# Newton steps of the FFN norms on VectorE, and pools that wait per tile, in a two-layer MLA/NSA decoder trunk

## The chip, the cores and the metric

The kernel runs on one core of a Trainium2 chip. A core has five engines that each work through a queue of their own in order: TensorE (PE, matmuls into PSUM banks), VectorE (DVE), ScalarE (ACT), GpSimd (POOL) and SyncE (SP, which here issues transfers). The metric is the device time of one execution in microseconds (us); the median of the runs before is 1926.41 us.

## The reference

The reference is a decoder trunk of depth 2 on one sequence of 512 tokens and 1024 channels, in float32. Each layer is

```
h = h + 0.5 * swiglu(rmsnorm(h, g_a), w_gate, w_up, w_down)
h = h + mixer(rmsnorm(h, g_m))
h = h + 0.5 * swiglu(rmsnorm(h, g_b), w_gate, w_up, w_down)
```

with `swiglu(x) = (silu(x @ w_gate) * (x @ w_up)) @ w_down` (2816 hidden channels) and `rmsnorm(x, g) = x * rsqrt(mean(x * x) + 1e-6) * g`. The mixer of layer 0 is multi-head latent attention (MLA, 16 heads), that of layer 1 native sparse attention (NSA: compressed, selected and sliding-window branches with gates and a relative bias). A last rmsnorm follows.

## The kernel before, in words

The hidden state lies in SBUF with channels on the partitions, as eight chunks `h` of 128 x 512. Six stages follow each other: FFN, MLA, FFN, FFN, NSA, FFN. Every float32 matmul is made of three matmuls on a high and a low part of each operand (L162 to L164, L364 to L366, L352 to L354 by stage). So every weight slab is loaded by SP into a buffer `wr` or `ru`, copied to a high part `w` by ACT (L143, L170) and its low part is made by DVE as the difference (L145, L171), or by POOL in the attention loops (L149). The slabs `w` have two buffers.

An FFN stage (`ffn`) computes the first three blocks of 128 hidden channels plainly (`plain`, two slabs each, gate into `pg` and up into `pu`), and the other 19 blocks by a scheme with seven products on combined operands (`combine` makes the combined inputs `four` from `h` with the operations L232, L236 to L238 and L171; `wsums` makes the sums of weights). The down projection runs in units of three blocks whose weights are `wd` (L407, L170, L171); the last four blocks are the tail, after which each chunk's square sum is added (L250 on ACT, L254 on POOL) and its input to the next stage is split (L173, L174).

The channel norm is not applied to the input of the matmuls; its factor per token, `row`, multiplies their results. It is made so: `norm_col` (L278) sums the squares over the partitions by four small matmuls into `pc`; `rsqrt` makes an estimate by three DVE steps (L259 to L261) and refines it by three Newton rounds on a tile of 128 x 4; `norm_bcast` (L290) spreads the result over all partitions by eight small PE instructions into `pb`; ACT copies `pb` to `row` (L450 in the FFN), and the gates `tg` are multiplied with it (L377). In the FFN `pb` stands in PE's order behind the second plain block. The Newton rounds of `rsqrt` have two forms:

```
for _ in range(3):
    if pool:
        nc.gpsimd.tensor_tensor(t, y, y, op=ALU.mult)                                # L264
        nc.gpsimd.tensor_tensor(t, t, v, op=ALU.mult)                                # L265
        nc.gpsimd.tensor_scalar(t, t, -0.5, 1.5, op0=ALU.mult, op1=ALU.add)          # L266
        nc.gpsimd.tensor_tensor(y, y, t, op=ALU.mult)                                # L267
        continue
    nc.vector.scalar_tensor_tensor(t, y, -0.5, v, op0=ALU.mult, op1=ALU.mult)        # L269
    nc.vector.tensor_tensor(t, t, y, op=ALU.mult)                                    # L270
    nc.vector.scalar_tensor_tensor(y, t, 1.5, y, op0=ALU.add, op1=ALU.mult)          # L271
```

The first FFN gets its square sums from token rows that ACT squares (L422), the others from `norm_col`. The norms of MLA and NSA call `rsqrt` without `pool`.

Tiles come from pools. Pools that live throughout hold `h`, the inputs (`x`, `four`), the weight slabs and small things; each stage opens pools of its own and releases them at its end: `act` and `ft` in an FFN, `mla` and `mlat` in MLA, `nsa`, `nsaq`, `cmp` (compression of keys and values, released inside the stage) and then `nsat` in NSA. Pools of a later stage lie on the bytes of earlier ones. `cmp` holds the bias table `btab` and its source `tb`, the positions `pos` (copied to `xc`, L950), the compression weights `w1` and `w2` (L962, L974), the hidden values and `vc`, which POOL copies into `vcm` (L1012). `nsat` holds `npth` and `nptl`, `th` (bias rows `cb`, L1031, and `th`, L1081, loaded from the table in DRAM), `e` (scores plus bias, L1038, transposed by PE into `ptc`, L1043), `p` and the outputs. The compressed scores `sc` are made at L1035 and L1036.

The program is recorded in the order of the Python code; the compiler then orders each engine's queue from a model of when each instruction can start, with earlier code first among those that are ready. A dependence on a released pool counts there like any other.

Of the kernel before, what the change touches and what calls it, by code (L numbers as in the profile page):

```python
# [20 lines left out]
D = 1024  # L21
# [40 lines left out]
class Kern:  # L62
# [305 lines left out]
    def ffn(self, idx, gain_next, ap, tp):  # L368
# [5 lines left out]
        def gate(f, g):  # L374

            t = tg[f] = tp.tile([P, S], F32, tag="tg", bufs=2, name="tg")
            nc.vector.tensor_tensor(t, g, row, op=ALU.mult)  # L377
            nc.scalar.activation(t, t, AF.Silu, scale=-1.0)
            nc.vector.tensor_tensor(t, t, row, op=ALU.mult)
# [4 lines left out]
        def act(f):  # L384
            t = tu[f]
            if f < PLAIN:
                t = tu_tile()
                nc.vector.scalar_tensor_tensor(t, tu[f], -1.0, tg[f], op0=ALU.mult, op1=ALU.mult)
            else:
                nc.vector.tensor_tensor(t, t, tg[f], op=ALU.mult)  # L390
            ah[f] = ap.tile([P, S], F32R, tag="act", bufs=4 * NG, name="ah")
            al[f] = ap.tile([P, S], F32R, tag="act", bufs=4 * NG, name="al")
            self.split(t, ah[f], al[f])
# [19 lines left out]
        sums, xts = self.small_sums, []  # L413

        def tokens(t):

            xts.append(tp.tile([P, D], F32, tag="fr", bufs=3, name="xt"))
            with self.tc.issue_after(self.high.ins):
                nc.scalar.dma_start(xts[t], a["x_tok"][t * P : (t + 1) * P, :])

        def squares(t):
            nc.scalar.activation(xts[t], xts[t], AF.Square, accum_out=sums[:, t : t + 1])  # L422
# [7 lines left out]
        for f, g in enumerate(gates):  # L430
            u = tu[f] = self.bank(("mm", "S")[f % 2], "pu")
            self.plain(idx, f, 0, g)
            if f == 1 and idx == 0:

                squares(0)
                tokens(3)
                squares(1)
            self.plain(idx, f, 1, u)
            if f == 0:
                for c in self.late:  # L440
                    self.sumsq(self.h[c])
                col = self.norm_col(D, self.s2, pool=True) if idx else None
            elif f == 1:
                if idx == 0:
                    squares(2)
                    squares(3)
                    col = self.rsqrt_col(sums, D, pool=True)
                pb = self.norm_bcast(col)
                row = tp.tile([P, S], F32, tag="row", bufs=1, name="row")
                nc.scalar.activation(row, pb, AF.Copy)  # L450
                for e in range(2):
                    gate(e, gates[e])
                    act(e)
            else:
                gate(f, g)
                act(f)
            for p in (((0,), (1,), (2, 3)) if idx else ((0, 1), (2,), (3,)))[f]:
                self.combine(p)
# [182 lines left out]
    def mla(self, gain_next):  # L641
        nc, tc, a = self.nc, self.tc, self.a
        with ExitStack() as cx:
            mp = cx.enter_context(tc.tile_pool(name="mla", bufs=1))
            tp = cx.enter_context(tc.tile_pool(name="mlat", bufs=2))
            self.chain, self.chained = None, True
            self.scr = tp, "p", 6
            cst = mp.tile([P, S], F32, name="cst")
# [184 lines left out]
    def nsa(self, gain_next):  # L833
        nc, tc, a = self.nc, self.tc, self.a
        with ExitStack() as cx:
            mp = cx.enter_context(tc.tile_pool(name="nsa", bufs=1))
            qp = cx.enter_context(tc.tile_pool(name="nsaq", bufs=1))
            rvalid = self.gains[:, 53:57]
            gat = mp.tile([P, 4, 3 * H], F32, name="gat")
            gcmp = mp.tile([P, 4, H], F32, name="gcmp")  # L840
# [91 lines left out]

            ks, vs, qs, pc, th, bank = {}, {}, [], {}, {}, {}

            with tc.tile_pool(name="cmp", bufs=1) as bp:
                self.chain, self.chained = None, True
                bt = self.bias_table(bp)
                for t in vcm:
# [39 lines left out]
                col = self.norm_col(D, self.s2)  # L978
# [36 lines left out]
                    nc.scalar.activation(gat[:, j, :], pv[j][:, 256:VG], AF.Sigmoid, scale=col[:, j : j + 1])  # L1015
                nc.vector.tensor_tensor(gcmp, gat[:, :, 0 : 3 * H : 3], rvalid[:, :, None].to_broadcast([P, 4, H]), op=ALU.mult)

            tp = cx.enter_context(tc.tile_pool(name="nsat", bufs=2))

            pths, ptls = [tp.tile([P, 2 * PTN], F32R, tag=x, bufs=1, name=x) for x in ("npth", "nptl")]  # L1020
            pth, ptl = [[t[:, br * PTN : br * PTN + PTN] for br in range(2)] for t in (pths, ptls)]
# [163 lines left out]
    def run(self):  # L1185
        tc = self.tc
        nxt = ["m0", "b0", "a1", "m1", "b1", "fin"]
        step = 0
        self.begin()
        for layer in range(2):  # L1190
            for which in range(3):
                if which == 1:
                    (self.mla, self.nsa)[layer](nxt[step])
                else:
                    with tc.tile_pool(name=f"act{step}", bufs=1) as ap, tc.tile_pool(name=f"ft{step}", bufs=2) as tp:
                        self.ffn(2 * layer + which // 2, nxt[step], ap, tp)
                step += 1

# [102 lines left out]
```

## Time and profile before

| what | value |
| --- | --- |
| median of 3 runs | 1926.41 us (1923.17 to 1928.86) |
| span of the profiled execution | 1920.1 us |
| PE busy | 1876.1 us, 98% |
| DVE busy | 1518.9 us, 79% |
| ACT busy | 1091.4 us, 57% |
| POOL busy | 334.9 us, 17% |
| mean granted clock of PE | 0.996 |
| moved by DMA | 183.28 MB, mean 95 GB/s |

The profile is of one execution, from its first instruction to its last; the time of a run also holds what lies around that. In a row of a timeline stand start and duration in us, engine, line, operation, the tile written and the tiles read, the shape, and in brackets the time for which the engine had been idle and what ended it. "q" behind an engine is its queue issuing a transfer. In the table by windows the pairs behind the length are busy us and number of instructions of PE, PE's weight load, DVE, ACT and POOL, then come the granted clock, DMA's share and GB/s.

### The profile page before, as it was taken

How to read it: one execution, taken by the hardware profiler on the slowest of the kernel's cores; microseconds unless marked ns; L12 is line 12 of the kernel's file. 1: busy time of each engine (PE TensorE's matmuls, PEld its weight loads, DVE VectorE, ACT ScalarE, POOL GpSimd, SP SyncE). 2: the span in 40 equal slices, each digit the busy share in tenths (PEclk: the TensorE clock that was granted, in tenths of full speed). 3: DMA queues.
4: the chain of work that ended last, by engine and by line, in shares of the span. 5: the costliest groups of instructions: out<-in, count | busy, mean ns of one | idle time of the engine just before them, and what ended most of it. 6: DMA issues, size and time to landing. Idle time of an engine off the chain costs nothing. (4 is left out here: it accounts for less than half of the span.)

```text
span 1920.1 us, 33220 instructions
## 1 busy us (share of the span) xinstructions
PE 1876.1 (98%) x12584; PEld 1707.3 (89%) x12584; DVE 1518.9 (79%) x2838; ACT 1091.4 (57%) x2040; POOL 334.9 (17%) x421
## 2 busy tenths in 40 slices
PE   8999999999999999999999999999999999999998
PEld 8999999878888999998999999877788888999997
DVE  7988886678778888876888888655987978888885
ACT  7555554478665555555555555435877865555553
POOL 1000000257631000002200000114666531000000
PEclk9999999999999999999999999999999999999999
DMA  6433321311233333323333332243122133333321
GB/s 224 140 100 99 113 90 42 110 50 42 73 116 111 100 100 109 112 62 107 117 110 108 104 100 79 65 123 100 51 67 67 40 118 96 108 112 108 104 76 67
DMA packets 75904, 183.28 MB, mean 95 GB/s; under 512 B 9040, under 2 KB 37072, under 8 KB 75744
## 3 DMA queue, kind: packets, MB, share of 16 engines
q1 hardware_dynamic: 72800, 176.39, 29.6%
q10 hardware_dynamic: 2944, 4.77, 0.7%
q8 instruction: 99, 1.62, 0.3%
q14 instruction: 61, 0.50, 0.1%
HBM read 178.96 MB, written 2.16 MB: 94 GB/s over the span
## 5 line engine op out<-in xcount | busy, mean ns | idle before, releaser
L254 POOL TENSOR_TENSOR s<-s,sq 128x512 f32<-128x512 f32 x38 | 55.7, 1466 | 988.2 <-ACT sq L250 985.2
L163 PE MATMUL pd<-al,wd 128*128 128x512 f32 x576 | 225.0, 391 | 0.0
L162 PE MATMUL pd<-ah,wd 128*128 128x512 f32 x576 | 224.8, 390 | 0.0
L164 PE MATMUL pd<-ah,wd 128*128 128x512 f32 x576 | 224.6, 390 | 0.0
L171 DVE TENSOR_TENSOR w<-wr,w 128x1024 fp32r<-128x1024 f32 x72 | 88.1, 1224 | 134.1 <-ACT w L170 134.1
L352 PE MATMUL px<-four,wh 128*128 128x256 f32 x608 | 168.5, 277 | 0.0
L354 PE MATMUL pq<-four,wl 128*128 128x256 f32 x608 | 167.9, 276 | 0.3 <-DVE wl L171 0.3
L354 PE MATMUL px<-four,wl 128*128 128x256 f32 x608 | 168.0, 276 | 0.0
L353 PE MATMUL px<-four,wh 128*128 128x256 f32 x608 | 167.9, 276 | 0.0
L352 PE MATMUL pq<-four,wh 128*128 128x256 f32 x608 | 167.9, 276 | 0.0
L353 PE MATMUL pq<-four,wh 128*128 128x256 f32 x608 | 167.8, 276 | 0.0
L143 ACT ACTIVATE w<-wr 128x1024 fp32r<-128x1024 f32 (+5 forms) x120 | 100.6, 844 | 104.7 <-issue 20.1
L401 DVE SCALAR_TENSOR_TENSOR h<-pd,h 128x512 f32<-128x512 f32 x216 | 148.0, 685 | 13.8 <-PE pd L164 13.7
L170 ACT ACTIVATE wd<-wdr 128x384 fp32r<-128x384 f32 x192 | 99.3, 519 | 101.4 <-ACT wd L170 62.9
L164 PEld LDWEIGHTS pd<-ah,wd 128*128 128x128 f32 x576 | 108.2, 188 | 22.9
L162 PEld LDWEIGHTS pd<-ah,wd 128*128 128x128 f32 x576 | 108.1, 188 | 20.3
L163 PEld LDWEIGHTS pd<-al,wd 128*128 128x128 f32 x576 | 108.1, 188 | 19.7
L145 DVE TENSOR_TENSOR w<-wr,w 128x1024 fp32r<-128x1024 f32 (+4 forms) x81 | 83.3, 1031 | 48.8 <-ACT w L143 48.2
L171 DVE TENSOR_TENSOR wd<-wdr,wd 128x384 fp32r<-128x384 f32 x192 | 105.7, 552 | 18.6 <-ACT wd L170 18.3
L639 ACT ACTIVATE p<-p,small 128x512 f32<-128x512 f32 (+1 forms) x192 | 106.8, 558 | 21.0 <-DVE small L638 17.3
L352 PEld LDWEIGHTS px<-four,wh 128*128 128x128 f32 x608 | 114.1, 188 | 0.9 <-ACT pg L477 0.5
L354 PEld LDWEIGHTS pq<-four,wl 128*128 128x128 f32 x608 | 114.1, 188 | 0.7 <-DVE wl L171 0.7
(359 smaller groups left out, 6281.1 us busy)
## 6 DMA issues: line engine op xcount, KB each, us to landing
wr<-in_w_gu SPq DMA_DIRECT2D x96, 512.0 KB, 3.3
ru<-in_w_gu SPq DMA_DIRECT2D x76, 512.0 KB, 4.2
wdr<-in_w_down SPq DMA_DIRECT2D x192, 192.0 KB, 2.4
wr<-in_w_down SPq DMA_DIRECT2D x24, 256.0 KB, 2.6
wr<-in_mla_w_o SPq DMA_DIRECT2D x8, 512.0 KB, 3.3
wr<-in_nsa_w_q SPq DMA_DIRECT2D x8, 512.0 KB, 3.3
th<-btab_d SPq DMA_DIRECT2D x16, 256.0 KB, 3.6
wr<-in_nsa_w_o SPq DMA_DIRECT2D x8, 512.0 KB, 3.6
```

The costliest lines, as they stand in the source:

```text
L143: self.copied = nc.scalar.activation(wh[:, m], raw[:, m], AF.Copy)
L145: nc.vector.tensor_tensor(wl[:, m], raw[:, m], f32v(wh[:, m]), op=ALU.subtract)
L162: mm(out, wh, xh, start=first, stop=False)
L163: mm(out, wh, xl, start=False, stop=False)
L164: return mm(out, wl, xh, start=False, stop=last)
L170: nc.scalar.activation(hi, src, AF.Copy)
L171: (nc.gpsimd if pool else nc.vector).tensor_tensor(lo, src, f32v(hi), op=ALU.subtract)
L352: mm(out, wh[:, p], xh, start=first and p == 0, stop=False, skip_group_check=True)
L353: mm(out, wh[:, p], xl, start=False, stop=False, skip_group_check=True)
L354: mm(out, wl[:, p], xh, start=False, stop=last and p == KP - 1, skip_group_check=True)
L401: nc.vector.scalar_tensor_tensor(self.h[c], p, 0.5, self.h[c], op0=ALU.mult, op1=ALU.add)
L639: nc.scalar.activation(p_sb[:, :n], p_sb[:, :n], AF.Exp, bias=nm, scale=-1.0, accum_out=sm)
```

## The change

The norms of the four FFN stages call `rsqrt` without `pool`, so their three Newton rounds are nine instructions on DVE (L269 to L271) in place of twelve on POOL (L264 to L267). And every pool that a stage opens gets `reuse_waits="tile"`. By default ("pool") all tiles of a pool that lands on bytes of released pools wait for every user of those pools; with "tile" each tile waits only for the users of earlier tiles on its own bytes. If the compiler sees that it cannot follow a pool's users, it ignores the setting for that pool.

```
-                col = self.norm_col(D, self.s2, pool=True) if idx else None
+                col = self.norm_col(D, self.s2) if idx else None
...
-                    col = self.rsqrt_col(sums, D, pool=True)
+                    col = self.rsqrt_col(sums, D)
...
-            mp = cx.enter_context(tc.tile_pool(name="mla", bufs=1))
-            tp = cx.enter_context(tc.tile_pool(name="mlat", bufs=2))
+            mp = cx.enter_context(tc.tile_pool(name="mla", bufs=1, reuse_waits="tile"))
+            tp = cx.enter_context(tc.tile_pool(name="mlat", bufs=2, reuse_waits="tile"))
...
-            mp = cx.enter_context(tc.tile_pool(name="nsa", bufs=1))
-            qp = cx.enter_context(tc.tile_pool(name="nsaq", bufs=1))
+            mp = cx.enter_context(tc.tile_pool(name="nsa", bufs=1, reuse_waits="tile"))
+            qp = cx.enter_context(tc.tile_pool(name="nsaq", bufs=1, reuse_waits="tile"))
...
-            with tc.tile_pool(name="cmp", bufs=1) as bp:
+            with tc.tile_pool(name="cmp", bufs=1, reuse_waits="tile") as bp:
...
-            tp = cx.enter_context(tc.tile_pool(name="nsat", bufs=2))
+            tp = cx.enter_context(tc.tile_pool(name="nsat", bufs=2, reuse_waits="tile"))
...
-                    with tc.tile_pool(name=f"act{step}", bufs=1) as ap, tc.tile_pool(name=f"ft{step}", bufs=2) as tp:
+                    with tc.tile_pool(name=f"act{step}", bufs=1, reuse_waits="tile") as ap, tc.tile_pool(name=f"ft{step}", bufs=2, reuse_waits="tile") as tp:
```

## The prediction

> **What bounds the kernel now.** I read the page first, then the waits of TensorE (PE), then the timeline around each long wait, then the table by windows for the granted clock.
>
> ```profile
> span 1920.1 us, 33220 instructions
> ...
> PE   1876.1 (98%) x12584; PEld 1707.3 (89%) x12584; DVE 1518.9 (79%) x2838; ACT 1091.4 (57%) x2040; POOL 334.9 (17%) x421
> ```
>
> TensorE is busy for all but 44.0 us of the span, so a change that leaves its matmuls as they are, as this one does, can win only from those 44.0 us and from stretches in which matmuls run slowly. The waits of PE (total, times, longest) name them:
>
> ```profile
> PE pb L290 <- POOL small L267: 10.6, 4, 4.2
> ...
> PE pcm L164 <- DVE w L145: 2.2, 2, 1.7
> ...
> PE ptc L1043 <- issue: 1.7, 1, 1.7
> ```
>
> The longest is the broadcast pb of a channel norm, which waits for the last Newton step on GpSimd (POOL); it occurs in each of the four FFN stages. The pb rows of PE's timeline, in the order of the stages (in brackets the idle time before):
>
> ```profile
> 31.64 0.60 PE L290 MATMUL pb<-ident,small 128*128 128x128 f32 x3 [1.11 <-POOL small L267]
> ...
> 591.04 1.16 PE L290 MATMUL pb<-ident,small 128*128 128x128 f32 x8 [2.51 <-POOL small L267]
> ...
> 932.72 1.16 PE L290 MATMUL pb<-ident,small 128*128 128x128 f32 x8 [2.79 <-POOL small L267]
> ...
> 1591.08 2.07 PE L290 MATMUL pb<-ident,small 128*128 128x128 f32 x8 [4.18 <-POOL small L267]
> ```
>
> Start less idle time is when PE had run out of other work: 30.53, 588.53, 929.93 and 1586.90. Some of these waits cost more than themselves. In the table by windows the granted clock is the third column from the end:
>
> ```profile
> 588.00:598.00 10.00, 7.49 (x66) 7.29 (x65) 5.29 (x8) 4.33 (x6) 2.44 (x7) 1.00 0.34 107
> 930.00:940.00 10.00, 7.28 (x50) 7.28 (x50) 5.70 (x8) 4.11 (x6) 2.17 (x7) 0.83 0.38 125
> 1324.00:1331.00 7.00, 5.05 (x19) 4.06 (x20) 4.60 (x15) 3.71 (x8) 3.33 (x4) 0.76 0.77 260
> 1591.00:1597.00 6.00, 5.92 (x30) 5.92 (x31) 2.52 (x5) 3.03 (x4) 0.03 (x1) 0.56 0.28 90
> ```
>
> Matmul time lost to the clock is length times (1 - clock): 0 behind the 2.51 us wait, 10 x 0.17 = 1.7 us behind the 2.79, 6 x 0.44 = 2.6 us behind the 4.18, and 7 x 0.24 = 1.7 us behind the wait of ptc in the NSA stage.
>
> **Part one, the Newton steps.** Removed: 12 POOL instructions in each of four norms, each dependent on the one before. Why they take so long, from POOL's timeline in the second and the last FFN of layer 1:
>
> ```profile
> 921.72 6.65 POOL L264 TENSOR_TENSOR small<-small 128x4 f32<-128x4 f32 x1 [10.49 <-DVE small L261]
> ...
> 1580.30 6.39 POOL L264 TENSOR_TENSOR small<-small 128x4 f32<-128x4 f32 x1 [9.82 <-DVE small L261]
> 1586.76 0.20 POOL L265 TENSOR_TENSOR small<-small 128x4 f32<-128x4 f32 x1
> ...
> 1588.93 1.25 POOL L264 TENSOR_TENSOR small<-small 128x4 f32<-128x4 f32 x1
> ```
>
> The same 128x4 form takes 0.20 us or 6.39 us. VectorE (DVE) over the same time:
>
> ```profile
> 1580.06 0.16 DVE L261 TENSOR_SCALAR small<-small 128x4 int32<-128x4 int32 x1
> 1580.13 1.22 DVE L145 TENSOR_TENSOR w<-wr,w 128x1024 fp32r<-128x1024 f32 x1
> ...
> 1585.41 1.21 DVE L145 TENSOR_TENSOR w<-wr,w 128x1024 fp32r<-128x1024 f32 x1
> 1587.96 0.56 DVE L171 TENSOR_TENSOR wd<-wdr,wd 128x384 fp32r<-128x384 f32 x1 [1.34 <-ACT wd L170]
> 1588.91 1.23 DVE L145 TENSOR_TENSOR w<-wr,w 128x1024 fp32r<-128x1024 f32 x1 [0.39 <-ACT w L143]
> 1593.83 1.29 DVE L377 TENSOR_TENSOR tg<-pg,row 128x512 f32<-128x512 f32 x2 [3.69 <-ACT row L450]
> ```
>
> POOL's long step lasts exactly as long as DVE's unbroken run of two-input operations (to 1585.41 + 1.21 = 1586.62), and the 1.25 us step lies on the L145 of 1588.91: POOL reads only when DVE pauses. On DVE the steps cannot be shut out like that, but they queue. Added: 9 DVE instructions a norm. Their price is that of the same lines in the MLA norm, which already uses them:
>
> ```profile
> 359.84 1.23 DVE L145 TENSOR_TENSOR w<-wr,w 128x1024 fp32r<-128x1024 f32 x1
> 360.99 0.16 DVE L269 SCALAR_TENSOR_TENSOR small<-small 128x4 f32<-128x4 f32 x1
> ...
> 361.97 0.16 DVE L271 SCALAR_TENSOR_TENSOR small<-small 128x4 f32<-128x4 f32 x1
> ```
>
> Six steps start within 361.97 - 360.99 = 0.98 us, 0.196 us apiece, so nine take 1.8 us back to back. Where other DVE work is ready, the order puts one of its operations between two dependent steps, an L145 here, another L145 behind L261 above. Then a step costs the queue only 1580.13 - 1580.06 = 0.07 us, nine cost 0.6 us, and the chain's end is the end of the work between. Two prices for each stage follow: "woven" (the nine lie within the existing run) and "behind" (all nine come after it, 1.8 us). The ends of the run in the other stages:
>
> ```profile
> 28.21 0.68 DVE L236 TENSOR_TENSOR u<-y 128x512 f32<-128x512 f32 x1
> ...
> 29.42 0.41 DVE L237 TENSOR_TENSOR u<-y,u 128x256 f32<-128x256 f32 x1
> 29.75 1.21 DVE L171 TENSOR_TENSOR four<-u,four 128x1024 fp32r<-128x1024 f32 x1
> ...
> 586.69 1.22 DVE L145 TENSOR_TENSOR w<-wr,w 128x1024 fp32r<-128x1024 f32 x1
> ...
> 928.61 0.56 DVE L171 TENSOR_TENSOR wd<-wdr,wd 128x384 fp32r<-128x384 f32 x1 [0.29 <-ACT wd L170]
> ```
>
> - First FFN: the run ends at 30.96; its chain starts before that run, so woven it is done before PE wants it at 30.53 and the 1.11 us go. Behind: 32.8, which is 1.2 us later than today's pb.
> - Second: the run ends at 587.91; woven 588.5 to 588.8 against 588.53. I take 0.3 us left, a gain of 2.2; behind, 589.7, a gain of 1.3.
> - Third: the run ends at 929.17, woven 929.8 against 929.93; I take 0.1 left, a gain of 2.7; behind, 931.0, a gain of 1.7. With the 1.7 us of clock: 4.4.
> - Fourth: the run ends at 1586.62, woven 1587.2; I take 0.5 left, signal included, a gain of 3.7; behind, 1588.4, a gain of 2.7. With the 2.6 us of clock: 6.3.
>
> I take woven, since that is the order in which L261 and the MLA steps already lie. Sum: 1.1 + 2.2 + 4.4 + 6.3 = 14.0 us; the bounds are 8.8 (behind, clock recovered: -1.2 + 1.3 + 3.4 + 5.3) and 14.9 (nothing left: 10.6 + 1.7 + 2.6). Behind the nine steps in DVE's queue stand the weight splits L145 that PE needs; 0.6 us of delay is covered by DVE's idle 1.34 us in the row of 1587.96. What was late next, row and then tg (L377), follows pb by a fixed chain and moves up with it: DVE idles 3.69 us before it today. POOL has nothing else queued there.
>
> [...]
>
> **Part two, the pools.** Today a tile of a new pool waits for all users of the released pools under it; then only for users of its own bytes. No instruction is added; what moves up is transfers and preparation of the next stage. Two places show a price:
>
> ```profile
> 1317.72 3.13 POOL L1012 TENSOR_SCALAR vcm<-vc 32x128 fp32r<-32x128 f32 x9
> ...
> 1320.88 1.73 SPq L1031 DMA_DIRECT2D cb<-btab_d  x4
> ...
> 1324.60 0.69 DVE L1038 TENSOR_TENSOR e<-sc,cb 128x512 f32<-128x512 f32 x1 [2.46 <-DMA cb<-btab_d]
> ```
>
> The cb loads start the moment POOL's last reader of the pool "cmp" ends (1320.85); e waits for them and ptc for e. By the order in which the two pools request tiles, cb lies on a w1 buffer that was read long before, so cb can be there before its scores, and ptc's 1.7 us wait goes with its 1.7 us of clock: 3.4 us. Bounds 0 (SP's order or another wait holds it) and 3.4.
>
> ```profile
> 1253.56 1.59 POOL L254 TENSOR_TENSOR s<-s,sq 128x512 f32<-128x512 f32 x1 [0.50 <-ACT sq L250]
> ...
> 1255.17 0.34 ACTq L819 DMA_DIRECT2D tb<-in_rel_bias  x1
> ...
> 1262.33 0.18 DVE L950 COPY xc<-pos 128x16 f32<-128x16 f32 x1 [2.07 <-DMA pos<-in_nsa_pos]
> 1262.42 1.22 DVE L145 TENSOR_TENSOR w<-wr,w 128x1024 fp32r<-128x1024 f32 x1
> ```
>
> At the start of NSA the small loads on ScalarE's queue wait for the last square sum (1255.15), pos lands late, and L950 holds up in DVE's queue the split L145 for which PE waits 2.2 us (pcm, above). If pos is loaded earlier, most of it goes: 1.5 us, bounds 0 and 2.2.
>
> At the three entries into a later FFN, FFN preparation may now run inside the stage before. DVE there:
>
> ```profile
> 880.00:902.00 22.00, 22.00 (x98) 18.20 (x98) 16.03 (x24) 12.36 (x20) 5.36 (x4) 1.00 0.25 72
> 545.00:564.00 19.00, 18.76 (x89) 15.79 (x90) 16.40 (x18) 11.35 (x18) 7.36 (x6) 1.00 0.32 94
> ```
>
> DVE (third pair) is 16.03 of 22 and 16.40 of 19 us busy, PE full. A 1.2 us operation placed ahead of a weight split can make PE wait. I take 0.5 us lost at each, 1.5; between a gain of 1.7 (a wait on a split as long as the pcm row's longest goes) and the loss that the last rival prices.
>
> Together 14.0 + 3.4 + 1.5 - 1.5 = 17.4 us: a span of 1902.7, and since the median is 6.3 us above the profiled span, 1926.4 - 17.4 = 1909.0 us. A measurement of this kernel can tell about 0.3% (5.8 us) from no change.
>
> **The rivals.**
> - Steps behind the run, not woven: 8.8 in place of 14.0, 1914.2 us. For it: L269 to L271 followed each other undivided in the row group of 360.99 to 361.97. Against: no other work was ready there. Chance 0.10.
> - The pools do nothing for PE, or the change is ignored there because the compiler cannot follow a pool's users: 14.0 alone, 1912.4 us; with the 1.5 lost, 1913.9. For it: PE's waits show only 3.9 us that pools explain. Chance 0.15.
> - [...] Chance 0.08.
> - Another wait ends last at pb, such as PE's own weights behind a delayed L145: the 10.6 us come back elsewhere, and 0 to 5 us remain, 1921 to 1926. DVE's idle 3.69 us speaks against it. Chance 0.05.
> - Slower: preparation runs ahead of the splits at all three entries. One FFN's combinations take 4 x (0.68 + 2 x 0.41 + 1.21) = 10.8 us of DVE, and two splits of weight sums and two of unit weights 2 x 1.22 + 2 x 0.56 = 3.6 more, 14.4 in all. Against DVE's spare time (6.0 at the FFN tail, 2.6 at each of two w_o tails) that is 8.4 + 11.8 + 11.8 = 32 us of PE waiting at most, 1926.4 - 18.9 + 32 = 1939.5 us. It decides for slower once over 18.9 + 5.8 = 24.7 of the 32 are lost. Against it: the order favours the earlier stage's work when both are ready. Chance 0.05.
>
> **How the numbers follow.** The forecast has 0.57, the rivals 0.43. The range of 1903 to 1919 holds the forecast with its bounds (best: 14.9 + 3.4 + 2.2 + 1.7 = 22.2, 1904) and the first three rivals with some loss at the entries; the last two lie outside. Faster by over 0.3%, under 1920.6: 0.89; within: 0.06; slower: 0.05.
>
> **What would show it.** Right: no pb row with over 1 us of idle time; granted clock 1.00 behind all four; nine L269 to L271 rows per FFN norm among L145 and L171; no wait at ptc and cb issued before 1313 on today's scale. Wrong: pb waiting for DVE L271 by over 1.5 us (behind); PE waiting on L145 for over 2 us in an FFN tail or w_o (hoisting); cb still behind L1012 (pools without effect).

## The result and the profile after

The changed kernel takes 1903.24 us (median of 4 runs, 1902.31 to 1904.29) beside 1925.87 us for the kernel before (4 runs, 1923.17 to 1928.86): a ratio of 0.9887, with a 95% interval of 0.987 to 0.9904. It is faster, and its time lies 5.8 us below the forecast of 1909.0.

The page of the kernel after begins so (span and instructions, then busy time, share of the span and instructions of each engine):

```profile
span 1902.5 us, 33162 instructions
...
PE 1871.4 (98%) x12584; PEld 1703.2 (90%) x12584; DVE 1523.5 (80%) x2874; ACT 1090.6 (57%) x2040; POOL 303.5 (16%) x373
```

The span fell by 1920.1 - 1902.5 = 17.6 us. DVE has 36 instructions more (4 x 9), POOL 48 fewer (4 x 12). The page's own mean clock went from 0.996 to 0.998. Next the waits of PE after (total, times, longest):

```profile
PE pg L364 <- ACT w L143: 6.0, 1, 6.0
PE pb L290 <- DVE small L271: 2.0, 3, 1.2
PE s L1103 <- DVE small L638: 1.6, 2, 0.8
PE s L1085 <- DVE small L638: 1.3, 3, 0.7
PE ptc L1060 <- POOL e L1055: 1.0, 1, 1.0
...
PE pcm L164 <- DVE w L145: 0.5, 1, 0.5
```

The 10.6 us at `pb` behind POOL are gone, the 2.2 us at `pcm` are down to 0.5, and the row "ptc L1043" of 1.7 us is not there at all. The first row is PE's wait for the first weights at the start of the run, 5.8 us before; the change doesn't touch it. Next to what is left at `pb` now stand the waits for NSA's softmax (L638, L1055).

Where the 17.6 us come from is read by setting PE's timeline of both kernels side by side at the same instructions. The marks of before that the prediction doesn't show are the square-sum matmuls `pc` of three FFNs, the first plain product after `pb` in the third FFN, the start of NSA, and the last transposes:

```profile
574.98 0.95 PE L278 MATMUL pc<-ones,s 128*128 128x1 f32 x8
...
917.97 0.95 PE L278 MATMUL pc<-ones,s 128*128 128x1 f32 x8
...
946.23 0.28 PE L352 MATMUL px<-x,w 128*128 128x256 f32 x1
...
1248.79 0.39 PE L162 MATMUL pcm<-x,w 128*128 128x512 f32 x1
...
1325.39 0.63 PE L1043 MATMUL ptc<-ident,e 128*128 128x128 f32 x4 [1.70 <-issue]
...
1335.50 0.66 PE L1060 MATMUL ptc<-ident,e 128*128 128x128 f32 x4 [0.96 <-POOL e L1055]
...
1574.83 0.95 PE L278 MATMUL pc<-ones,s 128*128 128x1 f32 x8
...
1886.19 2.04 PE L500 MATMUL ph<-ident,h 128*128 128x128 f32 x16
```

The same rows of the kernel after, with its four `pb`:

```profile
31.21 1.16 PE L290 MATMUL pb<-ident,small 128*128 128x128 f32 x8
...
574.25 0.95 PE L278 MATMUL pc<-ones,s 128*128 128x1 f32 x8
...
587.80 1.13 PE L290 MATMUL pb<-ident,small 128*128 128x128 f32 x8
...
914.15 0.94 PE L278 MATMUL pc<-ones,s 128*128 128x1 f32 x8
...
925.95 1.05 PE L290 MATMUL pb<-ident,small 128*128 128x128 f32 x8
...
937.74 0.28 PE L352 MATMUL px<-x,w 128*128 128x256 f32 x1
...
1240.80 0.39 PE L162 MATMUL pcm<-x,w 128*128 128x512 f32 x1
...
1313.63 0.60 PE L1043 MATMUL ptc<-ident,e 128*128 128x128 f32 x4
...
1323.20 0.66 PE L1060 MATMUL ptc<-ident,e 128*128 128x128 f32 x4 [1.05 <-POOL e L1055]
...
1562.70 0.95 PE L278 MATMUL pc<-ones,s 128*128 128x1 f32 x8
...
1575.94 1.13 PE L290 MATMUL pb<-ident,small 128*128 128x128 f32 x8 [1.17 <-DVE small L271]
...
1868.59 1.60 PE L500 MATMUL ph<-ident,h 128*128 128x128 f32 x12
```

Each section is the distance between two marks, after less before:

| section | us |
| --- | --- |
| start to the first FFN's `pb` | -0.43 |
| to the second FFN's `pc` | -0.30 |
| second FFN, `pc` to `pb` | -2.51 |
| to the third FFN's `pc` | -0.58 |
| third FFN, `pc` to `pb` | -2.95 |
| third FFN, `pb` to `px` | -1.72 |
| to `pcm` at the start of NSA | +0.50 |
| `pcm` to the first `ptc` | -3.77 |
| to the fourth FFN's `pc` | -0.37 |
| fourth FFN, `pc` to `pb` | -3.01 |
| fourth FFN, `pb` to `ph` | -2.46 |
| sum | -17.60 |

The two rows "`pb` to ..." are the granted clock: PE is busy for the whole of these stretches in both kernels (13.51 and 11.79 us, 295.11 and 292.65 us), at a clock of 0.87 and 0.99 before and of 1.00 after. The same table by windows as before, after the four long waits' places (clock third from the end):

```profile
588.00:598.00 10.00, 10.00 (x90) 10.00 (x90) 8.01 (x12) 7.27 (x12) 0.00 (x0) 1.00 0.34 107
926.00:936.00 10.00, 10.00 (x90) 10.00 (x90) 8.51 (x13) 6.15 (x11) 0.00 (x0) 1.00 0.47 145
1312.00:1319.00 7.00, 5.52 (x26) 4.15 (x27) 5.42 (x16) 4.99 (x9) 4.47 (x5) 1.00 0.80 260
1576.00:1582.00 6.00, 6.00 (x53) 6.00 (x54) 4.83 (x7) 3.11 (x5) 0.00 (x0) 1.00 0.69 227
```

Where before had 1.00, 0.83, 0.76 and 0.56, it is 1.00 four times. DVE's timeline in the fourth FFN shows how the steps lie:

```profile
1567.93 0.16 DVE L261 TENSOR_SCALAR small<-small 128x4 int32<-128x4 int32 x1
1568.00 1.21 DVE L145 TENSOR_TENSOR w<-wr,w 128x1024 fp32r<-128x1024 f32 x1
1569.14 0.15 DVE L269 SCALAR_TENSOR_TENSOR small<-small 128x4 f32<-128x4 f32 x1
1569.21 1.21 DVE L171 TENSOR_TENSOR four<-u,four 128x1024 fp32r<-128x1024 f32 x1
1570.35 0.15 DVE L270 TENSOR_TENSOR small<-small 128x4 f32<-128x4 f32 x1
...
1575.64 0.16 DVE L271 SCALAR_TENSOR_TENSOR small<-small 128x4 f32<-128x4 f32 x1
```

One operation of other work stands between each two steps, and a step costs the queue 1569.21 - 1569.14 = 0.07 us. But the operation between sets the pace: the nine steps end at 1575.80, 6.66 us after the first began, and PE had run dry at 1575.94 - 1.17 = 1574.77.

In NSA the bias rows `cb` began to leave the queue at 1304.11, before POOL's last readers of the compression pool began at 1305.26, and all four were issued 5 us before these readers ended. SP's, POOL's and DVE's rows of after:

```profile
1304.11 1.81 SPq L1031 DMA_DIRECT2D cb<-btab_d  x4
...
1305.26 5.67 POOL L1012 TENSOR_SCALAR vcm<-vc 32x128 fp32r<-32x128 f32 x16 [1.56 <-DVE vc L171]
...
1311.96 0.68 DVE L1038 TENSOR_TENSOR e<-sc,cb 128x512 f32<-128x512 f32 x1
```

Before, `cb` left right behind the last L1012, and L1038 waited 2.46 us for it. Now L1038 shows no wait.

### The profile page after: what moved, and what is told of

It reads as the page before. It is cut to its first block, busy times and chain, and to the rows that moved or that the text cites. A ratio compares the mean times of both kernels' runs of the same rounds, so it can differ in the third digit from the quotient of the medians.

```text
span 1902.5 us, 33162 instructions
## 1 busy us (share of the span) xinstructions
PE 1871.4 (98%) x12584; PEld 1703.2 (90%) x12584; DVE 1523.5 (80%) x2874; ACT 1090.6 (57%) x2040; POOL 303.5 (16%) x373
## 3 DMA queue, kind: packets, MB, share of 16 engines
q8 instruction: 99, 1.62, 0.4%
## 4 chain that ended last, share of the span: by engine, by line
PE 60%; DVE 5%; ACT 2%; issue 1%; POOL 1%; DMA 1%; ACTq 0%; POOLq 0%; DVEq 0%
PE pd L163 6%; PE pd L162 6%; PE pd L164 6%; PE px L352 4%; PE px L353 4%; PE px L354 4%; PE pg L352 3%; PE pg L353 3%; PE pg L354 3%; PE pq L353 3%; PE pq L354 3%; PE pq L352 3%; PE o L604 1%; PE pt L593 1%; PE po L164 1%
## 5 line engine op out<-in xcount | busy, mean ns | idle before, releaser
L171 DVE TENSOR_TENSOR w<-wr,w 128x1024 fp32r<-128x1024 f32 x72 | 88.1, 1224 | 129.0 <-ACT w L170 129.0
L171 DVE TENSOR_TENSOR wd<-wdr,wd 128x384 fp32r<-128x384 f32 x192 | 106.5, 556 | 20.8 <-ACT wd L170 20.3
L145 DVE TENSOR_TENSOR w<-wr,w 128x1024 fp32r<-128x1024 f32 (+4 forms) x81 | 82.8, 1024 | 45.8 <-ACT w L143 45.1
```

Of the source, the lines that this page charges most:

```text
L145: nc.vector.tensor_tensor(wl[:, m], raw[:, m], f32v(wh[:, m]), op=ALU.subtract)
L171: (nc.gpsimd if pool else nc.vector).tensor_tensor(lo, src, f32v(hi), op=ALU.subtract)
```

## The experiments

The theory at this point: the gain is that of two independent parts. The Newton steps free `pb` and with it the clock behind it; the pools free `pcm` and `ptc` in NSA. The rivals are that one part does it all (pools without effect, or Newton waits replaced by others), and that the median's distance from the profile is something other than half clocks. The first four runs shared one chip with 23 runs of the kernel before (median 1923.87 us).

**One part alone (e1_newton_only, e2_pools_only).** The first keeps the Newton steps and takes `reuse_waits` out of all the pools; the second does the opposite:

```
e1:
-            mp = cx.enter_context(tc.tile_pool(name="mla", bufs=1, reuse_waits="tile"))
+            mp = cx.enter_context(tc.tile_pool(name="mla", bufs=1))
...
e2:
-                col = self.norm_col(D, self.s2) if idx else None
+                col = self.norm_col(D, self.s2, pool=True) if idx else None
...
-                    col = self.rsqrt_col(sums, D)
+                    col = self.rsqrt_col(sums, D, pool=True)
```

> The Newton steps of the four FFN norms on VectorE, all pools waiting as before. Theory (the gain is the sum of two independent parts, and the Newton part is the pb waits with their half clock): the four pb waits fall from 10.6 us to under 2.5 us, no half clock behind them, span 1920.1 - 13.5 = 1906 to 1908; the waits of pcm (2.2 us) and ptc (1.7 us, clock 0.76 behind it) stay. Rival (the pools carry it, since preparation that moves up empties VectorE before the Newton steps): the pb waits keep more than half of their 10.6 us, span above 1913.

> All stage pools wait per tile, the Newton steps stay on GpSimd. Theory: the pb waits stay at 9 to 11 us with half clock behind at least one of them, pcm's wait falls under 1 us and ptc's goes, span 1920.1 - 5 = 1914 to 1917. Rival (pools carry it): pb waits under 5 us, span under 1911.

Measured: Newton alone 1911.62 us (6 runs, 1908.62 to 1914.93; ratio 0.9945, 0.9928 to 0.9962), pools alone 1917.22 us (12 runs, 1914.07 to 1923.07; ratio 0.997, 0.9957 to 0.9984). The waits of PE with Newton alone:

```profile
PE pcm L164 <- DVE w L145: 2.5, 2, 2.1
PE pb L290 <- DVE small L271: 2.1, 3, 1.3
PE ptc L1043 <- issue: 1.5, 1, 1.5
```

and with the pools alone:

```profile
PE pb L290 <- POOL small L267: 10.7, 4, 4.3
```

where `pcm` has 0.4 us left and "ptc L1043" no row. Each part removes its own waits and leaves the other's. The gains in the medians are 1923.87 - 1911.62 = 12.25 and 1923.87 - 1917.22 = 6.65 us. The span of Newton alone, 1909.7 us in the profile, lies above the 1906 to 1908 expected. Its mean clock is 0.997, beside 0.998 for the profile of after, and by an estimate from these two figures and the spans (0.003 x 1909.7 and 0.002 x 1902.5) it lost about 1.9 us more to the clock than after; its longest wait of `pcm` is 2.1 us, 1.7 in before.

**Both again, and before again (e3_after_again, e4_before_again).** No edit; they give the sum on the same chip and a second profile of each kernel.

> The changed kernel once more, beside the two halves on the same chip. Theory: 1902 to 1905 us, as before; the gains of the two halves in time add up to its gain within 3 us. Rival (the halves overlap, one makes the other superfluous): the sum of the two gains exceeds its gain by more than 5 us.

> The kernel before, unchanged, so that every run of it lists its span and clock. The profiled execution of before had a span of 1920.1 us, the timed runs a median of 1925.9; of the changed kernel each run lies 1.8 us above its span. Theory (the half clock behind PE's waits comes and goes from run to run): spans between 1920 and 1927 at granted clocks between 0.996 and 0.993, the longer the lower the clock. Rival (the difference lies outside the span): spans near 1920 with times 4 to 6 us above them.

Measured: 1904.92 us (6 runs; ratio 0.9907, 0.9891 to 0.9923), a gain of 18.95 beside 12.25 + 6.65 = 18.90: the parts add up. That they meet so closely is chance, since the interval of each ratio leaves some 3 us to its gain. The kernel before measured 1925.0 us (12 runs, 1919.41 to 1931.09; ratio 1.0007, 0.9992 to 1.0022). Of the 35 runs of before in these rows, the time is the span plus 1.7 to 1.9 us in every one, and the span itself goes from 1916.7 us to 1929.3 us with a mean clock from 0.997 down to 0.991. The span of after goes from 1900.4 to 1904.0. So the kernel before is not 6.3 us longer outside its span: its span differs from run to run, and the profiled one was among the short ones.

**Which pools (e7_newton_nsa_pools, e8_newton_ffn_pools).** All Newton steps on DVE; per-tile waits in the NSA pools alone, or in the FFN and MLA pools alone. The edit of e7, and that of e8 in its pattern:

```
e7:
-            mp = cx.enter_context(tc.tile_pool(name="mla", bufs=1, reuse_waits="tile"))
+            mp = cx.enter_context(tc.tile_pool(name="mla", bufs=1))
...
e8:
-            with tc.tile_pool(name="cmp", bufs=1, reuse_waits="tile") as bp:
+            with tc.tile_pool(name="cmp", bufs=1) as bp:
...
-            tp = cx.enter_context(tc.tile_pool(name="nsat", bufs=2, reuse_waits="tile"))
+            tp = cx.enter_context(tc.tile_pool(name="nsat", bufs=2))
```

> Newton steps on VectorE, waits per tile only for the four pools of the NSA stage. Theory (what the pools are worth lies in NSA, at pcm and ptc): 4 to 5 us less than with the Newton steps alone, 1906 to 1909; pb at the NSA norm and the first ptc gain as in the changed kernel. Rival (half of it lies at the entries of the FFN stages): 2 to 3 us less than Newton alone, 1909 to 1911.

> Newton steps on VectorE, waits per tile only for the FFN and MLA pools. Theory: 1 to 2.5 us less than with the Newton steps alone (1.2 us at the entry after MLA), pcm and ptc wait as before, 1909 to 1911. Rival (preparation that moves into the stages before costs there what it gains): within 1 us of Newton alone, or slower.

Measured: 1905.63 us with the NSA pools (5 runs, 1904.04 to 1907.15; ratio 0.9897, 0.9884 to 0.991) and 1908.65 us with the others (5 runs, 1907.67 to 1910.2; ratio 0.9916, 0.9904 to 0.9928). The waits of PE in the second of them:

```profile
PE pcm L164 <- DVE w L145: 2.5, 2, 2.0
...
PE ptc L1043 <- issue: 1.6, 1, 1.6
```

The two waits stay unless NSA's own pools change, and its clock table shows 0.76 over 1316 to 1323, behind `ptc`. Against Newton alone (1911.62, on another chip) the NSA pools are worth 6.0 us and the FFN and MLA pools 3.0, both more than expected; together that is more than the 1911.62 - 1904.92 = 6.7 of all the pools by e3. On e7's and e8's own chip the next experiment, e5, is the kernel after plus a chain that nobody waits for, at 1903.86 us. Against it the lack of the NSA pools costs 1908.65 - 1903.86 = 4.8 us and that of the others 1905.63 - 1903.86 = 1.8, in all 6.6. So the NSA pools are worth the larger part, and the FFN and MLA pools lose nothing.

**The cause of POOL's long step (e5_shadow).** The kernel after, with an extra Newton chain on POOL whose result nobody uses, beside the same DVE work; in the third FFN twelve `memset`s stand in its place.

```
+            for _ in range(3):
+                if self.shadow == 2:
+                    for x in (1.0, 2.0, 3.0, 4.0):
+                        nc.gpsimd.memset(z, x)
+                    continue
+                nc.gpsimd.tensor_tensor(u, z, z, op=ALU.mult)
...
```

> The changed kernel, plus a chain on GpSimd in the later three FFN norms that nobody waits for, started from a copy of the estimate (one more small VectorE instruction) when VectorE's own steps start. In the second and fourth FFN it is the twelve old Newton instructions, which read SBUF; in the third it is twelve memsets of the same 128x4, which only write. Theory (GpSimd's reads are shut out by VectorE's run of two-input operations): the first reading instruction lasts 3 us or more in the second and fourth FFN, the chain 6 us or more, while no memset in the third lasts over 0.5 us and its chain under 4 us. Rival (GpSimd is slow to start after its 10 us of idle time, or slow by itself): the first memset lasts 3 us or more too. Both: time within 2 us of the changed kernel, since no engine waits for the chain.

Measured: 1903.86 us (2 runs), a span of 1901.5. POOL's rows, the third FFN first and then the fourth (its lines are moved down by the edit):

```profile
918.48 1.85 POOL L269 MEMSET shd<- 128x4 f32 x12 [11.67 <-DVE small L282]
...
1568.42 1.20 POOL L271 TENSOR_TENSOR shd<-shd 128x4 f32<-128x4 f32 x1 [11.02 <-DVE small L282]
...
1572.55 1.14 POOL L272 TENSOR_TENSOR shd<-shd,small 128x4 f32<-128x4 f32 x1
...
1574.85 0.20 POOL L271 TENSOR_TENSOR shd<-shd 128x4 f32<-128x4 f32 x1
```

The twelve memsets take 1.85 us together, 0.15 us apiece, though POOL had been idle for 11.67 us: a slow first step after a pause is ruled out for steps that write only, and the reading step after the pause (1.20 us) is no longer than a later one without a pause (1.25 us at 1575.12). The steps that read take from 0.19 to 1.25 us; the longest are about as long as one split L145 on DVE (1.21 to 1.23 us in the fourth FFN of after). The first reading step was expected to last 3 us or more, and that did not happen: the 6.39 us step of before does not come back beside a DVE run that now has a small step after nearly every operation (the rows of after above). That POOL gets in at these small steps is the author's reading of the lengths. The chain of twelve still takes 8.5 us (1568.42 to 1576.93), as expected.

**How much the chain's length counts (e6_twice).** Six Newton rounds in place of three in the FFN norms, which adds nine steps to each.

```
-        for _ in range(3):
+        for _ in range(6 if self.twice else 3):
```

> The changed kernel with six Newton rounds in place of three in the four FFN norms (18 VectorE steps; more rounds give the same factor). Theory (the end of the chain of steps sets pb, and a wait there risks a half clock of 3.4 us): the added nine steps come after VectorE's run, 0.2 us each or behind one more operation; pb waits of 1.5 to 3.5 us in each of the four FFN, 7 to 12 us in all, half clock in some of them, time 1911 to 1917. Rival (pb is not what TensorE's next work waits for, the weight splits are): pb waits under 4 us in all, time under 1907.

Measured: 1909.14 us (6 runs, 1907.02 to 1912.76; ratio 0.992, 0.9907 to 0.9932). PE's wait (lines moved by one):

```profile
PE pb L291 <- DVE small L272: 8.3, 6, 2.6
```

The four FFN waits are 1.65, 1.81, 1.43 and 2.57 us where after has 0, 0, 0 and 1.17. In the fourth the added nine steps follow the last woven one back to back, from 1579.06 to 1580.79, 0.19 us a step, and 2.57 - 1.17 = 1.4 us of their 1.73 reach PE. The half clock that was expected behind some of them did not come (mean clock 0.999; behind the 2.57 us wait the 128x256 matmuls take 0.28 us each, as in front of it), and the time stayed under the 1911 to 1917 expected; what the profiles show of this is in the section on the hardware. The time rose by 1909.14 - 1903.86 = 5.3 us over e5, the nearest kernel to after on its chip; the waits sum to 8.3 - 1.9 = 6.4 us more than in e5. In the fourth FFN a step that finds no partner costs its 0.19 us, most of it on the path: this is the price that the rival "behind" would have paid.

**Can the rest be had (e9_chain_first, e10_after_third).** In the fourth FFN 1.17 us were left because each step waited for the operation woven before it. Here the weight sums of the first product block and the down units beside it are issued behind the last Newton step, so fewer operations can be woven in; e10 is the kernel after, on the same chip.

```
-            nc.vector.scalar_tensor_tensor(y, t, 1.5, y, op0=ALU.add, op1=ALU.mult)
+            self.newton = nc.vector.scalar_tensor_tensor(y, t, 1.5, y, op0=ALU.add, op1=ALU.mult)
...
-            w = self.wsums(idx, f)
+            with self.tc.issue_after(self.newton.ins) if f == PLAIN else nullcontext():
+                w = self.wsums(idx, f)
...
-                work(tag)
+                with self.tc.issue_after(self.newton.ins) if f == PLAIN else nullcontext():
+                    work(tag)
```

> The changed kernel, with the first weight sums and the first down units of an FFN ordered on VectorE behind the last Newton step, so that fewer long operations lie between the steps. Theory (what is left of the pb waits is the woven order): the 1.2 us wait of the fourth FFN falls under 0.3 us and no new wait of over 0.5 us comes up behind it; about 1 us less than the changed kernel on the same chip, too little to tell by time. Rival (the first products of the scheme then wait for their weights): a new wait at px or pq in the later FFN stages, time 2 us or more above the changed kernel.

> The changed kernel once more beside it: 1902 to 1906 us, granted clock 0.998 or 0.999 in every run, since no wait of PE in it is long enough for a half clock; the kernel before on the same chip spreads over 0.991 to 0.997.

Measured: 1900.99 us (4 runs, 1899.36 to 1904.51; ratio 0.987, 0.9853 to 0.9887) beside 1903.35 us (4 runs, 1902.92 to 1903.78; ratio 0.9879, 0.9862 to 0.9896). The first two rows are DVE's and the last is PE's, all in the fourth FFN of e9:

```profile
1564.80 0.15 DVE L269 SCALAR_TENSOR_TENSOR small<-small 128x4 f32<-128x4 f32 x1
...
1567.59 0.15 DVE L271 SCALAR_TENSOR_TENSOR small<-small 128x4 f32<-128x4 f32 x1
...
1570.96 1.05 PE L290 MATMUL pb<-ident,small 128*128 128x128 f32 x8
```

The chain now takes 1567.74 - 1564.80 = 2.94 us in place of 6.66 and ends 3.2 us before PE wants it: no FFN's `pb` waits. That the residue came from weaving is thereby shown. A new wait came up in the second FFN, where `px` waits 0.6 us for ACT's `pg` (L478); that is a trace of what the rival expected, far from its price. In the profiles the span is 4.4 us shorter (1902.0 and 1897.6), of which PE's waits at `pb` explain 1.6 (2.4 and 0.8 in all); the rest is not assigned. In the medians it is 2.4 us, and the intervals overlap, so that it beats the kernel after is likely and not settled.

## Why the prediction was right, and what in it was off

The mechanism held in the main, and the span was forecast at 1902.7 where 1902.5 came; but this closeness hides errors that cancel. The time lies at the very edge of the forecast's range, 0.2 us inside it, and the measured gain of 1925.87 - 1903.24 = 22.6 us is more than the 22.2 of its best case: that the range still holds it is luck. By time on one chip the Newton steps gave 12.25 us for the 14.0 forecast and the pools 6.65 for 3.4 (3.4 + 1.5 - 1.5); what follows goes by the sections of the two profiles.

**Newton steps: 14.0 forecast, 13.1 measured** (0.43 + 2.51 + 2.95 + 1.72 + 3.01 + 2.46 of the table). "Woven" was the right choice over "behind": the rows show it, and e6 shows what appended steps cost. By stage: first FFN 0.43 for 1.1, second 2.51 for 2.2, third 4.67 for 4.4, fourth 5.47 for 6.3. The step that was mis-sized is "0.5 left" in the fourth, measured 1.17: the steps' cost to the queue was priced (0.07 us each), but not that each of them waits for the operation woven before it. The old run ends 11.8 us after `pc` in both kernels (1586.62 - 1574.83 and 1574.47 - 1562.70); only six of the nine steps lie within it, and the last three come behind it with two L171 between them. So the prediction's own sign of being right, no `pb` with over 1 us of idle time, was missed here by little. In the first FFN the wait differs between profiles of the same kernel by more than the term: it is 0 in the profile above and 1.79 us in e3's. There the prediction's "woven it is done before PE wants it at 30.53" failed. The chain begins when ACT has squared the last token row; in after ACT waited 1.37 us for that row's transfer and got it at 25.66 us, the chain ended at 31.16, and PE wanted it at 31.21. In e3 PE wanted the chain's end at 31.00 and started `pb` at 32.79. So it is luck that the wait is 0 in the profile of after.

**Start of NSA and `ptc`: 1.5 + 1.7 forecast without clock, 3.77 measured.** `pcm`'s wait fell from 2.2 to 0.5 us, 1.7 for 1.5, and `ptc`'s from 1.7 to nothing; 0.4 us of the section is not assigned to a wait. e8 ties both waits to NSA's pools. The way was the forecast one: `pos` is issued at 1244.67 and 1245.63, before the last square sum on POOL ends (1245.62 + 1.58 = 1247.20), and L950's waits for it fall from 8.2 to 2.2 us in all.

**The half clock behind `ptc`: 1.7 forecast, at most 0.54 measured.** This is the failed term of "3.4". The clock did return to 1.00, yet the next wait on POOL's `e` (`ptc` L1060) came 1335.50 - 1325.39 = 10.11 us after the first `ptc` before and 1323.20 - 1313.63 = 9.57 us after, and the whole section to the fourth FFN's `pc` gained 0.37. The rows show why the faster matmuls brought so little. PE is busy for 8.58 of the 10.11 us before and for 7.39 of the 9.57 after; of the 1.19 us of matmul time saved, 2.18 - 1.53 = 0.65 came back as idle time, because in this stretch PE ends up waiting for the softmax (`s` and `ptc` L1060 behind DVE and POOL, both before and after). So of the 1.19 us that the slow clock cost in matmul time only 0.54 came back as time: here it counted only as far as PE was the bound.

**Entries into later FFNs: 1.5 lost forecast, none measured.** The sections with the entries into the second and the third FFN are 0.30 and 0.58 us shorter, and the one with the entry into the fourth is the 0.37 named above. The sign was wrong and the size small. The only loss, 0.50 us between `px` of the third FFN and `pcm`, lies before the start of NSA and is not assigned to a wait. The rival "slower" has nothing left: no wait of PE for L145 of over 0.8 us appears in the list of after, and e8 is not slower than e1.

**From span to time: the step that cost 4.5 of the 5.8 us.** The prediction took the 6.3 us between the median and the profiled span as lying outside the span, and carried them over to the changed kernel. The runs show 1.7 to 2.0 us there, for every kernel. By that the other 4.5 were the runs of before, whose spans were longer than the profiled one. By 1902.7 + 1.8 the forecast would have been 1904.5, beside 1903.24. The mean clock tells the two kernels' runs apart: 0.991 to 0.997 for before, 0.998 to 0.999 for after.

**The other rivals.** "Pools do nothing" falls with e2 (6.65 us by themselves); "another wait ends last at `pb`" with the rows of `pb`; that the half clocks are not due to the short waits falls with the four clocks of 1.00 and the next section.

## What the runs showed of the hardware

**The half clock starts on a grid.** In the profile of before the granted clock is 0.50 from 934.10, from 1326.63 and from 1589.46 us (and once more behind PE's last matmul). These starts lie 392.53 and 262.83 us apart, which is 115 and 77 times 3.413 us, and the stretches last 3.41, 3.41 and 6.83 us, one period or two. So the windows can be laid on that grid; the table by windows (PE's busy time is the first number behind the length):

```profile
589.35:592.77 3.42, 1.73 (x15) 1.73 (x16) 1.22 (x1) 0.86 (x2) 1.47 (x3) 1.00 0.59 189
592.77:596.18 3.41, 3.41 (x33) 3.41 (x32) 2.65 (x5) 2.50 (x4) 0.00 (x0) 1.00 0.26 102
930.69:934.10 3.41, 1.38 (x12) 1.38 (x13) 1.23 (x1) 0.57 (x2) 1.72 (x4) 1.00 0.68 219
934.10:937.51 3.41, 3.41 (x19) 3.41 (x18) 2.87 (x5) 1.64 (x3) 0.00 (x0) 0.50 0.26 100
```

A window with 3.42 - 1.73 = 1.69 us idle is followed by full clock, one with 3.41 - 1.38 = 2.03 us by half. Seven windows at full clock inside the run of before, behind the first weights, have over 1 us of idle time: those with 1.96, 2.03 and 2.56 us were followed by half clock, those with 1.03, 1.11, 1.69 and 1.72 us by full. Of windows between 1.72 and 1.96 us this profile has none. One window at half clock already, with 3.41 - 1.79 = 1.62 us idle (from 1589.46), was followed by half clock again. A full period at half clock loses 3.41 / 2 = 1.7 us of matmul time.

So in this profile it depended on the grid whether a wait of 2 to 3 us cost clock: the 2.51 us wait before the second `pb` lost nothing (0.82 us of it lay in the preceding window, 1.69 in the next), while of the 2.79 us before the third 2.03 lay in one window. In e2 the same two waits, 2.51 and 2.79 us, ended alike: behind the first the 128x256 matmuls take 0.28 us each, behind the second 0.41. In e6 the wait of 2.57 us cost no clock; how it lay on the grid its rows do not show.

The spread of the kernel before goes with its clock: at a mean clock of 0.997 its span is 1916.7 us and at 0.991 it is 1929.3, and by an estimate from these figures (0.003 x 1916.7 = 5.8 and 0.009 x 1929.3 = 17.4) 11.6 of the 12.6 us between them go to the clock. The kernel after, whose waits before `pb`, `pcm` and `ptc` were at most 1.79 us (e3), has in its profile a clock of 1.00 from 12.2 to 1896.3 us, behind its last matmul, and a mean of 0.998 or 0.999 in every run, and its span varies by less than 4 us.

**POOL's first reading step lasted to the end of DVE's run of two-input operations in three FFNs; the writing steps of e5 took 0.15 us apiece.** In the second FFN of before POOL's step lasted 3.18 us, to 585.07, and DVE's run ended at 585.01; in the third it lasted 6.65 us, to 928.37, and the run ended at 928.32; in the fourth it lasted 6.39 us, to 1586.69, and the run ended at 1586.62. The twelve memsets of e5 took 1.85 us in all; they ran beside a run with small steps in it, in which no reading step took more than 1.25 us either, so a writing step beside an unbroken run was not shown. Nor did a reading step always wait for a pause. In the second FFN of before POOL's L267 lasted from 585.72 to 586.83 and ended between two DVE operations that followed each other without a pause, an L171 to 586.77 and an L145 from 586.69. What let it in there and not in the longer runs stays open.

## What to carry to other kernels

In the kernel before, waits that left PE idle for 1.96 to 2.56 us of one 3.41 us period were followed by one or two periods at half clock (1.7 us of matmul time each), by chance of where they fell; ones that left 1.03 to 1.72 us were not. With those waits gone, the half clock behind them and most of the run-to-run spread went too (12.6 us of span before, 3.6 after), so compare the span and the clock of every run before taking a profiled span for the typical one. Small dependent steps that the scheduler weaves into a run of large operations cost the queue little (0.07 us each here), but their chain goes at the pace of the large ones (6.66 us for nine); when the chain's end is waited for, order the large ones behind it (2.94 us in e9). Price a recovered clock only where the matmuls and not a softmax on other engines set the pace (1.19 us of matmul time saved brought 0.54 here).
